# Retention's last values in one narrow run, folded squares for the last keys and queries, masks in other buffers

## The chip, the cores and the metric

The kernel runs on one core of a Trainium2 chip. The metric is the device time of one execution in microseconds (us). Before the change it is 1216.12 us, the median of three runs (1215.96 to 1216.55).

## The reference

An encoder of two layers on 512 tokens of width 1024, all in float32. In each layer one projection of the normed input feeds two groups of heads: eight heads of retention in both directions, and four heads of differential attention. Both are projected back and added, and a SwiGLU network follows. What this change touches:

```python
# retention, per head, in its closed form
# out[t] = sum_{s<=t} gf^(t-s) (q_t.k_s) v_s + sum_{s>t} gb^(s-t) (q_t.k_s) v_s
ret = rms_norm(ret, ret_norm_g[l]) * jax.nn.silu(rg)      # per head of 64

# differential attention: keys and queries are normed per head of 64
dqn = rms_norm(dq, dq_norm_g[l]) * DIFF_HEAD_DIM ** -0.5
dkn = rms_norm(dk, dk_norm_g[l])
...
x = x + concat([ret, da]) @ w_out[l]
```

## The kernel before

Activations lie transposed: 128 features on the partitions, 512 tokens along the free dimension. Most products are made of three passes in a rounded float32 format: an operand is split into a rounded part `hi` and a rest `lo`, and `mm3` (L220) issues hi*hi, hi*lo and lo*hi. The splits cost a cast on ScalarE (ACT) and a subtraction on VectorE (DVE).

Retention works on pairs of heads, 0 to 3, in two chunks of 256 tokens. For a pair, `prepare` weighs queries and keys by the decay and stacks their parts (with moves issued by SP); `scores` multiplies queries and keys of each chunk into the `sc` banks (L581) and multiplies them by the decays into mask tiles `sm` (L587); `state` makes the 64x64 state between chunks (L502); `cross` applies it to the queries (L514); `values` multiplies masks and values (L525); `norm` norms the result, multiplies it by the gate and splits it into a part of the mix, which the output projection's second half reads. `state`, `cross` and `values` are plain float32 matmuls, and `state` and `values` are narrow: they use 64 columns of the array, two at a time side by side.

The order in this stage is written out as the string `STEPS` (L38): `a`, `b` and `n` with a number are `prepare`, `scores` and `norm` of a pair, `k` is `state`, `v` and `V` are `cross` and `values`, `+` joins several into one run, `h` is the end of the last attention head, and `-` takes the next piece of other work (projections, then the output projection's first half from the attention heads). `together` chains the matmuls of a run one behind the other with order edges, all crosses first. With `V` the weighing of that pair's queries is put behind the other things that the run needs. `scores` puts its matmuls behind the run before it, and pair 3's decays behind the first matmul of the run before. The string and these edges give rank and order; a planner in the framework then places each instruction on its engine, by rank, as its inputs and buffers come free, and may move later work forward.

The four attention heads run before that stage. `heads` gives sixteen turns (four a head), and `weave` puts one piece of a list between two turns: keys and queries of heads 2 and 3 (`project_k`, `project_q`), the four gates, and the first retention projections. A `yield` in a piece hands over to the next turn. `qk_tile` norms keys or queries: `square_sums` squares the tile, splits it, and adds over each head's 64 rows with two matmuls (L140 and L141) against a matrix of ones. `fold` and `folded_sums` do the same for an attention head's output with one matmul (L162): an accumulating DMA on POOL adds the upper 64 rows of squares to the lower 64, and hi and lo of the sums are stacked in one tile.

Buffers are pools by tag: `ah` has 4, `h` has 8 (the normed input of the layer, and later that of the second norm), `w` has 12, `mix` 20.

Of the kernel before, what the change touches and what calls it, by code (L numbers as in the profile page):

```python
# [8 lines left out]
F32 = mybir.dt.float32  # L9
F32R = mybir.dt.float32r  # L10
AF = mybir.ActivationFunctionType
ALU = mybir.AluOpType

P = 128
D = 1024
T = 512
DEPTH = 2
KT = D // P
HD = 64
# [15 lines left out]
PLAIN = FFN[0][1]  # L35
BEGUN, LASTS = (2, 9, 10, 20, 21), (18,)

STEPS = "a0 h - b0 - a1 - - - - k0+k1 b1 - - a2 - - a3 V0+v1+k2+k3 b2 b3 n0 n1 - - - V2 n2 - - v3 - n3"  # L38


NW, NQK, NMIX, NAH, NHL = 12, 11, 20, 4, 3
# [4 lines left out]
PRM_AG, PRM_FG, PRM_RG, PRM_QG, PRM_KG, PRM_DG = 0, 16, 32, 34, 36, 38  # L46
# [9 lines left out]
def encoder_kernel(ctx: ExitStack, tc: tile.TileContext, xT, xg, wfirst, wsingle, wvv, wout, wgu, wdn, wds, prm, lam, cst, outT):  # L56
    nc = tc.nc
# [4 lines left out]
    tpool = ctx.enter_context(tc.tile_pool(name="tpool", bufs=1))  # L62
# [5 lines left out]
    def nm(s):  # L68
        uid[0] += 1
        return f"{s}{uid[0]}"  # L70

    def big(s, dt=F32, tag="w", bufs=NW):
        return tpool.tile([P, T], dt, tag=tag, name=nm(s), bufs=bufs)
# [17 lines left out]
    consts, first_part = {}, []  # L91

    def f32(ap):
        return ap.bitcast(F32)
# [18 lines left out]
    prm_sb = cpool.tile([P, PRM_N], F32, name="prm_sb")  # L113
# [23 lines left out]
    def column_sums(ps, w, src):  # L137

        hi, lo = split(src, "w", NW)
        sums[1] = nc.tensor.matmul(ps, w, hi, start=True, stop=False).ins.name  # L140
        sums[0] = nc.tensor.matmul(ps, w, lo, start=False, stop=True).ins.name  # L141
# [3 lines left out]
    def square_sums(ps, w, src):  # L145
        sq = big("sq")
        nc.scalar.activation(sq, src, AF.Square)
        column_sums(ps, w, sq)
        return sq
# [8 lines left out]
    def folded_sums(ps, w, sq):  # L158
        parts = big("hl", F32R)
        nc.scalar.copy(parts[:HD], sq[:HD])  # L160
        nc.vector.tensor_tensor(parts[HD:], sq[:HD], f32(parts[:HD]), op=ALU.subtract)
        nc.tensor.matmul(ps, w, parts, start=True, stop=True)  # L162

    def round_ones():
        o = big("ones")
# [71 lines left out]
    def split(src, tag, bufs):  # L237
        hi, lo = pair() if tag == "h" else [big(n, F32R, tag, bufs) for n in ("hi", "lo")]
        casts[0] = nc.scalar.copy(hi, src).ins.name
        splits[0] = nc.vector.tensor_tensor(lo, src, f32(hi), op=ALU.subtract).ins.name  # L240
        return hi, lo
# [3 lines left out]
    def rsqrt(out, src, scale):  # L245

        func(out, src, AF.Ln, bias=eps_sb, scale=scale)
        func(out, out, AF.Exp, scale=-0.5)
# [84 lines left out]
    def layer(l, n1, h, x_src, first_raw):  # L333
# [27 lines left out]
        lg, nlgb, lamn, gq, gd, wk, rs = (consts[k] for k in ("lg", "nlgb", "lamn", "gq", "gd", "wk", "rs"))  # L361
# [43 lines left out]
                k.append((hi, lo))  # L405
            return k

        def qk_tile(u, col, early, stack):
            ss = aux_bank()
            sq = square_sums(ss, consts["bones_r"], u)  # L410
            rsqrt(sq, ss, 1.0 / HD)

            nc.vector.scalar_tensor_tensor(u, u, col, sq, op0=ALU.mult, op1=ALU.mult)
            nc.scalar.activation(sq, sq, AF.Square, scale=HD ** -0.5)
            nc.vector.scalar_tensor_tensor(sq, ss, HD * EPS, sq, op0=ALU.add, op1=ALU.mult)
            nc.vector.scalar_tensor_tensor(u, sq, 3.0, u, op0=ALU.subtract, op1=ALU.mult)
            return stack(u, *(("qk", NQK) if early else ("mix", NMIX)))
# [54 lines left out]

        ret, run = [dict() for _ in range(4)], [None, None]

        def together(steps):
            names = [n for t in steps for n in (ret[int(t[1])]["state" if t[0] == "k" else "values"])]
            ins = [i for t in steps if t[0] != "k" for i in cross(int(t[1]))]
            ins += [i for t in steps for i in (state if t[0] == "k" else values)(int(t[1]))]
            for i, before in zip(ins, [names] + [[i.name] for i in ins]):
                for name in before:  # L480
                    tc.add_manual_dep(i, name, order, reason="one run of plain matmuls")
            if steps[0][0] == "k":
                tc.add_manual_dep(ins[0], scored[0], order, reason="one run of plain matmuls")
            run[:] = ins[-1].name, ins[0].name
            first = [ret[int(t[1])]["weigh"] for t in steps if t[0] == "V"][:1]
            for i in first:
                for name in names:
                    if name != i.name:
                        tc.add_manual_dep(i, name, order, reason="one run of plain matmuls")
# [69 lines left out]
        def scores(pr):  # L559
            lgc = lambda d, hh: lg[:, l * 16 + d * 8 + 2 * pr + hh : l * 16 + d * 8 + 2 * pr + hh + 1]  # L560
            lgm = lambda hh: nlgb[:, l * 8 + 2 * pr + hh : l * 8 + 2 * pr + hh + 1]
            qs, ks = ret[pr]["stacks"]
            both = []

            for hh in range(2):
                arg = big("arg")
                i = nc.scalar.activation(arg[:, :384], signed, AF.Copy, scale=lgm(hh))
                if run[1] and pr == 3:
                    tc.add_manual_dep(i.ins, run[1], order, reason="decays behind the run")
                nc.vector.scalar_tensor_tensor(arg[:, :384], signed, lgc(0, hh), arg[:, :384], op0=ALU.mult, op1=ALU.min)  # L570
                func(arg[:, :384], arg[:, :384], AF.Exp)
                both.append(bass.AP(arg.tensor, arg.offset, [arg.ap[0], [P, 2], [1, C]]))
            s = ret[pr]["s"] = []
            for c in range(2):
                ps = [sc_bank() for _ in range(2)]
                for j in range(2):
                    for hh in range(2):
                        out = ps[hh][:, (1 - j) * C : (2 - j) * C]
                        sb, tb = slice((2 * c + j) * P, (2 * c + j + 1) * P), slice(c * C, (c + 1) * C)
                        for part in range(2):  # L580
                            i = nc.tensor.matmul(out, ks[hh][part][:, sb], qs[hh][:, tb], start=part == 0, stop=part == 1)  # L581
                            if run[0]:
                                tc.add_manual_dep(i.ins, run[0], order, reason="one run of plain matmuls")
                scored[0] = i.ins.name
                sm = tpool.tile([P, 2, T], F32, tag="ah", name=nm("sm"), bufs=NAH)
                for hh in range(2):
                    i = nc.vector.tensor_tensor(  # L587
                        sm[:, hh].rearrange("p (j t) -> p j t", j=2), ps[hh].rearrange("p (j t) -> p j t", j=2), both[hh], op=ALU.mult
                    )
                    ret[pr]["values"].append(i.ins.name)  # L590
                s.append(sm)

        def norm(pr):
            o, ss = ret[pr]["o"], aux_bank()
            sq = square_sums(ss, consts["bones_r"], o)
            rsqrt(sq, ss, 1.0 / HD)
            nc.vector.scalar_tensor_tensor(sq, o, prm_sb[:, PRM_RG + l : PRM_RG + l + 1], sq, op0=ALU.mult, op1=ALU.mult)
            nc.vector.tensor_tensor(sq, sq, gates[pr], op=ALU.mult)
            mix[pr] = split(sq, "mix", NMIX)

        kgc = consts["gk"][:, l : l + 1]
        dv = [[], []]
        rv = [[], []]
        rks, rqs, gates = [], [], []
# [60 lines left out]
        def project_k(m):  # L665
            ps = project("dk", m)
            if m != 2:
                yield
            u = big("u")
            nc.vector.tensor_tensor(u, ps, rstd, op=ALU.mult)  # L670
            if m == 2:
                yield
            k[m] = qk_tile(u, kgc, False, stack_two)

        def project_q(m):
            ps = project("dq", m)
            yield
            u = big("u")
            nc.vector.tensor_tensor(u, ps, rstd, op=ALU.mult)
            q[m] = qk_tile(u, gq[:, l, m : m + 1], False, stack_one)  # L680

        def project_gate(m):
            t = big("rgt", tag="rn", bufs=4)
# [5 lines left out]
        q, k = [None] * 4, [None] * 4  # L689
# [49 lines left out]
        n2, h2, x = Norm(), [], []  # L739
# [38 lines left out]
        )  # L778
        for step in STEPS.split():
            if step == "-":  # L780
                next(fill)
            elif step == "h":
                next(lasthead[0])
            elif step[0] in "kvV":
                together(step.split("+"))
            else:
                {"a": prepare, "b": scores, "n": norm}[step[0]](int(step[1]))
        for _ in fill:
# [10 lines left out]
        n3, h3 = Norm(), []  # L799
# [195 lines left out]
        a1 = PLAIN  # L995
# [45 lines left out]
        a0, a1 = FFN[-1]  # L1041
# [30 lines left out]
    n, h, raws = Norm(), [], []  # L1072
# [7 lines left out]
    for l in range(DEPTH):  # L1080
        if l:
            raws = [load_chunk(wfirst[l, c]) for c in range(4)]
        n, h = layer(l, n, h, xT if l == 0 else xscr, raws)
# [89 lines left out]
```

## Time and profile before

| | before |
|---|---|
| median of three runs | 1216.12 us |
| profiled execution, its time | 1216.29 us |
| profiled execution, its span | 1214.5 us |
| TensorE matmuls (PE), busy | 1210.0 us, 7631 instructions |
| VectorE (DVE), busy | 961.1 us |
| ScalarE (ACT), busy | 744.8 us |
| GpSimd (POOL), busy | 99.2 us |

The span is the time from the first to the last instruction in the trace; the execution's time has 1.8 us more around it. In the order of time a row gives start, duration, engine, line, operation, what it writes and reads, shape and count; consecutive instructions of one kind share a row. A matmul's shown duration is longer than its distance to the next one, since matmuls overlap. 128*64 in a matmul's row means 128 rows and 64 columns of the array. A row of a group ends with busy time, the mean time of one in ns, and the idle time of the engine ahead of it. The stage of retention lies at about 190 to 260 us in layer 0 and at about 795 to 860 us in layer 1.

### The profile page before, as it was taken

To read this page: it belongs to the slowest core of one execution; us is meant where nothing else is said; L and a number is where in the kernel's file an instruction comes from. 1 tells how busy PE (TensorE), PEld (TensorE's weight loads), DVE (VectorE), ACT (ScalarE), POOL (GpSimd) and SP (SyncE) were. 2 spreads that over 40 slices of the span, in tenths; PEclk is the share of its full clock that TensorE was granted. 3 is DMA by queue.
4 is the path that set the end of the run, shared out by engine and by line. 5 is a ranking of instruction groups with operands and counts; after the bars stand their busy time and mean duration, and the time that the engine had idled before them with its cause. 6 is when DMAs were issued, how large, how long until landed. Compare 5 with 4: busy or idle time off the path is not lost.

```text
span 1214.5 us, 19995 instructions
## 1 busy us (share of the span) xinstructions
PE 1210.0 (100%) x7631; PEld 1083.2 (89%) x7631; DVE 961.1 (79%) x1585; ACT 744.8 (61%) x1300; POOL 99.2 (8%) x116
## 2 busy tenths in 40 slices
PE   9999999999999999999999999999999999999998
PEld 7888888888899999999888888887888999999997
DVE  6899777778978888876648996777789788898763
ACT  6877667655456556655548776676554565666541
POOL 1000001210011111110000000011100011111100
PEclk9999999999999999999999999999999999999999
DMA  7222224773176786782532222357532757867822
GB/s 268 87 70 76 89 75 126 155 188 104 64 170 166 173 214 155 181 218 84 169 113 79 78 74 74 92 144 163 144 122 73 181 144 190 207 161 182 202 79 96
DMA packets 71520, 164.87 MB, mean 136 GB/s; under 512 B 6912, under 2 KB 17408, under 8 KB 71424
## 3 DMA queue, kind: packets, MB, share of 16 engines
q1 hardware_dynamic: 54064, 133.00, 35.5%
q0 software_dynamic: 16928, 30.15, 15.0%
q8 instruction: 60, 0.98, 0.3%
q10 hardware_dynamic: 432, 0.44, 0.1%
q14 instruction: 36, 0.29, 0.1%
HBM read 153.34 MB, written 4.19 MB: 130 GB/s over the span
## 4 chain that ended last, share of the span: by engine, by line
PE 99%; DMA 0%; ACT 0%; DVE 0%; issue 0%
PE acc L913 23%; PE sc L913 17%; PE acc L221 11%; PE acc L222 11%; PE acc L223 11%; PE o L223 3%; PE o L222 3%; PE o L221 3%; PE sc L221 3%; PE sc L222 3%; PE sc L223 3%; PE sc L432 2%; PE sc L581 1%; PE o L525 1%; PE aux L448 1%; PE aux L140 1%
## 5 line engine op out<-in xcount | busy, mean ns | idle before, releaser
L208 ACT CAST hi<-raw 128x1024 fp32r<-128x1024 f32 (+2 forms) x117 | 115.8, 993 | 121.9 <-PE sc L222 39.3
L214 DVE TENSOR_TENSOR lo<-raw,hi 128x1024 fp32r<-128x1024 f32 (+2 forms) x118 | 135.4, 1150 | 36.6 <-ACT hi L208 35.9
L221 PE MATMUL acc<-h,hi 128*128 128x512 f32 (+1 forms) x344 | 134.3, 393 | 0.5 <-ACT h L232 0.4
L223 PE MATMUL acc<-h,lo 128*128 128x512 f32 (+1 forms) x344 | 134.1, 390 | 0.0
L222 PE MATMUL acc<-h,hi 128*128 128x512 f32 (+1 forms) x344 | 133.8, 389 | 0.0
L913 PE MATMUL acc<-hi,hi 128*128 128x256 f32 x432 | 122.5, 284 | 0.0
L913 PE MATMUL acc<-hi,lo 128*128 128x256 f32 x432 | 122.2, 283 | 0.0
L913 PE MATMUL acc<-lo,hi 128*128 128x256 f32 x432 | 122.2, 283 | 0.0
L870 DVE TENSOR_TENSOR lo<-s,hi 128x1024 fp32r<-128x1024 f32 (+1 forms) x78 | 89.0, 1141 | 32.7 <-ACT hi L869 32.4
L870 DVE TENSOR_TENSOR lo<-raw,hi 128x1024 fp32r<-128x1024 f32 (+1 forms) x78 | 89.0, 1141 | 30.9 <-ACT hi L869 26.9
L869 ACT CAST hi<-s 128x1024 fp32r<-128x1024 f32 (+1 forms) x78 | 76.7, 983 | 51.5 <-PE acc L913 37.1
L869 ACT CAST hi<-raw 128x1024 fp32r<-128x1024 f32 (+1 forms) x78 | 76.5, 981 | 39.0 <-PE acc L913 18.8
L913 PEld LDWEIGHTS acc<-lo,hi 128*128 128x128 f32 x432 | 82.9, 192 | 0.1
L913 PEld LDWEIGHTS acc<-hi,hi 128*128 128x128 f32 x432 | 82.9, 192 | 0.1
L913 PEld LDWEIGHTS acc<-hi,lo 128*128 128x128 f32 x432 | 82.9, 192 | 0.0
L221 PEld LDWEIGHTS acc<-h,hi 128*128 128x128 f32 x344 | 64.6, 188 | 14.4 <-PE o L223 0.7
L223 PEld LDWEIGHTS acc<-h,lo 128*128 128x128 f32 x344 | 64.6, 188 | 13.2
L891 POOL DMA_DIRECT2D s<-in_wgu x36 | 43.3, 1203 | 404.7 <-DMA s<-in_wgu 186.3
L222 PEld LDWEIGHTS acc<-h,hi 128*128 128x128 f32 x344 | 64.7, 188 | 12.8 <-DVE h L234 0.2
L913 PE MATMUL sc<-b,s 128*128 128x256 f32 x480 | 69.3, 283 | 0.0
L913 PEld LDWEIGHTS sc<-b,s 128*128 128x128 f32 x480 | 62.8, 192 | 0.0
L107 ACT ACTIVATE sc<-sc,mx 128x512 f32<-128x512 f32 x64 | 46.1, 721 | 22.8 <-DVE mx L436 22.5
(276 smaller groups left out, 3533.8 us busy)
## 6 DMA issues: line engine op xcount, KB each, us to landing
s<-in_wgu SPq DMA_DIRECT2D x54, 512.0 KB, 5.5
s<-in_wgu POOLq DMA_DIRECT2D x36, 512.0 KB, 7.5
raw<-in_wgu SPq DMA_DIRECT2D x34, 512.0 KB, 5.3
raw<-in_wsingle SPq DMA_DIRECT2D x32, 512.0 KB, 3.5
raw<-in_wvv SPq DMA_DIRECT2D x18, 512.0 KB, 3.5
raw<-in_wgu SPq DMA_DIRECT2D x36, 256.0 KB, 3.6
s<-in_wds SPq DMA_DIRECT2D x24, 384.0 KB, 3.4
raw<-in_wout SPq DMA_DIRECT2D x16, 512.0 KB, 3.7
```

Source lines behind the costliest of these rows:

```text
L107: i = nc.scalar.activation(out, src, f, **kw).ins
L140: sums[1] = nc.tensor.matmul(ps, w, hi, start=True, stop=False).ins.name
L208: c = nc.scalar.copy(hi[:, s], raw[:, s])
L214: nc.vector.tensor_tensor(lo[:, s], raw[:, s], f32(hi[:, s]), op=ALU.subtract)
L221: first = nc.tensor.matmul(out, L[0], R[0], start=start, stop=False)
L222: nc.tensor.matmul(out, L[0], R[1], start=False, stop=False)
L223: nc.tensor.matmul(out, L[1], R[0], start=False, stop=stop)
L432: nc.tensor.matmul(ps, q[m][:, t], k[m][part], start=part == 0, stop=part == 1)
L869: last_cast[0] = nc.scalar.copy(hi, raw).ins.name
L870: last_split[0] = nc.vector.tensor_tensor(lo, raw, f32(hi), op=ALU.subtract).ins.name
L891: nc.gpsimd.dma_start(sums, blocks[:, 0::3], accum_op=ALU.add)
L913: mm = nc.tensor.matmul(ps[:, t], L[x1], R[x2], start=start and k + i == 0, stop=k == n // P - 1 and i == 2, skip_group_check=True)
```

## The change

It has four parts.

- `STEPS`: pair 2's scores (`b2`) move ahead of the first run `V0+v1+k2+k3`, and the values of pairs 2 and 3 (`V2` and `v3`, two runs with other work between them) become one run `V2+v3` behind pair 3's scores, the norms of pairs 0 and 1, and three pieces of the output projection. The mark `!` says that a run is held behind the last score matmul emitted so far; before, that held for the run `k0+k1` alone.
- The squares of keys and queries of head 3 (`m == 3`): `fold_each` squares, and two accumulating DMAs on POOL add rows 32 to 63 to rows 0 to 31 of each head's 64; `each_parts` casts, subtracts, and two moves on SP put the rest `lo` into the freed half. One matmul makes the sums. Each of these tiles gets two more `yield`s.
- Pairs 2 and 3 take their mask tiles `sm` from tag `h` instead of `ah`.
- In `norm`, the gate is multiplied by the result and its weight ahead of the root; one product remains behind it.

```diff
-STEPS = "a0 h - b0 - a1 - - - - k0+k1 b1 - - a2 - - a3 V0+v1+k2+k3 b2 b3 n0 n1 - - - V2 n2 - - v3 - n3"
+STEPS = "a0 h - b0 - a1 - - - - !k0+k1 b1 - - a2 - - a3 b2 !V0+v1+k2+k3 b3 n0 n1 - - - !V2+v3 n2 - - - n3"
...
+    def fold_each(src):
+
+        sq = big("sq")
+        nc.scalar.activation(sq, src, AF.Square)
+        for b in (0, HD):
+            nc.gpsimd.dma_start(sq[b : b + 32], sq[b + 32 : b + HD], accum_op=ALU.add)
+        return sq
+
+    def each_parts(sq):
+        parts, lo = big("hl", F32R), big("lo", F32R)
+        nc.scalar.copy(parts, sq)
+        nc.vector.tensor_tensor(lo, sq, f32(parts), op=ALU.subtract)
+        for b in (0, HD):
+            nc.sync.dma_start(f32(parts[b + 32 : b + HD]), f32(lo[b : b + 32]))
+        return parts
...
-        def qk_tile(u, col, early, stack):
+        def qk_tile(u, col, early, stack, folded=None):
             ss = aux_bank()
-            sq = square_sums(ss, consts["bones_r"], u)
+            if folded:
+                sq, parts = folded
+                nc.tensor.matmul(ss, consts["bones_r"], parts, start=True, stop=True)
+            else:
+                sq = square_sums(ss, consts["bones_r"], u)
...
-        def together(steps):
+        def together(steps, behind=False):
...
-            if steps[0][0] == "k":
+            if behind:
                 tc.add_manual_dep(ins[0], scored[0], order, reason="one run of plain matmuls")
...
-                sm = tpool.tile([P, 2, T], F32, tag="ah", name=nm("sm"), bufs=NAH)
+                sm = tpool.tile([P, 2, T], F32, name=nm("sm"), **(dict(tag="ah", bufs=NAH) if pr < 2 else dict(tag="h", bufs=8)))
...
         def norm(pr):
             o, ss = ret[pr]["o"], aux_bank()
             sq = square_sums(ss, consts["bones_r"], o)
+            nc.vector.scalar_tensor_tensor(gates[pr], o, prm_sb[:, PRM_RG + l : PRM_RG + l + 1], gates[pr], op0=ALU.mult, op1=ALU.mult)
             rsqrt(sq, ss, 1.0 / HD)
-            nc.vector.scalar_tensor_tensor(sq, o, prm_sb[:, PRM_RG + l : PRM_RG + l + 1], sq, op0=ALU.mult, op1=ALU.mult)
             nc.vector.tensor_tensor(sq, sq, gates[pr], op=ALU.mult)
...
-            if m == 2:
+            folded = None
+            if m == 3:
+                sq = fold_each(u)
                 yield
-            k[m] = qk_tile(u, kgc, False, stack_two)
+                folded = sq, each_parts(sq)
+                yield
+            elif m == 2:
+                yield
+            k[m] = qk_tile(u, kgc, False, stack_two, folded)
...
-            q[m] = qk_tile(u, gq[:, l, m : m + 1], False, stack_one)
+            folded = None
+            if m == 3:
+                sq = fold_each(u)
+                yield
+                folded = sq, each_parts(sq)
+                yield
+            q[m] = qk_tile(u, gq[:, l, m : m + 1], False, stack_one, folded)
...
-            elif step[0] in "kvV":
-                together(step.split("+"))
+            elif step[0] in "!kvV":
+                together(step.strip("!").split("+"), step[0] == "!")
```

## The prediction

> **What bounds the kernel now.** I read the page first (busy time, clock, chain), then the waits of TensorE, then the order of time around the stage that the change touches.
>
> ```profile
> span 1214.5 us, 19995 instructions
> PE 1210.0 (100%) x7631; PEld 1083.2 (89%) x7631; DVE 961.1 (79%) x1585; ACT 744.8 (61%) x1300; POOL 99.2 (8%) x116
> PEclk9999999999999999999999999999999999999999
> PE 99%; DMA 0%; ACT 0%; DVE 0%; issue 0%
> ```
>
> ```profile
> PE aux L118 <- PEq L1165: 0.8, 1, 0.8
> PE acc L221 <- ACT h L232: 0.4, 1, 0.4
> ```
>
> The chain that ended last is TensorE for 99%, the clock is granted in full in every slice, and in the whole program TensorE waits twice, both times at the start. So only two things can change the time: work that TensorE no longer has, and a wait that it gets. The busy column does not give the price of a matmul, because matmuls overlap; I take it from start to start in the order of time. I show layer 0; the same stage of layer 1 lies some 603 us later.
>
> This is the run of plain matmuls of pairs 0 and 1 with the states of pairs 2 and 3:
>
> ```profile
> 200.32 0.39 PE L223 MATMUL acc<-h,lo 128*128 128x512 f32 x1
> ...
> 221.77 0.39 PE L223 MATMUL acc<-hi,lo 128*128 128x512 f32 x1
> 222.00 1.89 PE L514 MATMUL o<-wq,rs 128*128 128x256 f32 x8
> 223.82 3.67 PE L525 MATMUL o<-sm,rv 128*64 128x256 f32 x32
> 227.32 1.10 PE L502 MATMUL aux<-rv,kw 128*64 128x64 f32 x32
> 228.35 0.39 PE L581 MATMUL sc<-q,khi 128*128 128x256 f32 x1
> ```
>
> These are one pair of squares' sums, then the values of pair 2 between two halves of pair 3's scores, then those of pair 3:
>
> ```profile
> 231.70 0.40 PE L140 MATMUL aux<-hi,bones_r 128*128 128x512 f32 x1
> 231.94 0.39 PE L141 MATMUL aux<-lo,bones_r 128*128 128x512 f32 x1
> 232.17 0.39 PE L222 MATMUL acc<-lo,hi 128*128 128x512 f32 x1
> ...
> 237.76 1.03 PE L514 MATMUL o<-wq,rs 128*128 128x256 f32 x4
> 238.72 1.95 PE L525 MATMUL o<-sm,rv 128*64 128x256 f32 x16
> 240.59 0.39 PE L581 MATMUL sc<-q,khi 128*128 128x256 f32 x1
> 240.82 0.28 PE L581 MATMUL sc<-q,klo 128*128 128x256 f32 x1
> 240.94 0.28 PE L581 MATMUL sc<-q,khi 128*128 128x256 f32 x1
> ...
> 241.72 1.03 PE L514 MATMUL o<-wq,rs 128*128 128x256 f32 x4
> 242.40 0.58 PE L140 MATMUL aux<-hi,bones_r 128*128 128x512 f32 x1
> 242.82 0.39 PE L221 MATMUL sc<-hi,hi 128*128 128x512 f32 x1
> ...
> 243.52 0.39 PE L221 MATMUL sc<-hi,hi 128*128 128x512 f32 x1
> 243.83 1.95 PE L525 MATMUL o<-sm,rv 128*64 128x256 f32 x16
> 245.71 0.50 PE L221 MATMUL sc<-hi,hi 128*128 128x512 f32 x1
> 246.04 0.40 PE L222 MATMUL sc<-lo,hi 128*128 128x512 f32 x1
> 246.28 0.40 PE L223 MATMUL sc<-hi,lo 128*128 128x512 f32 x1
> ```
>
> A wide matmul of 512 columns has a pitch of 0.23 us (231.94 to 232.17), one of 256 columns 0.12 us (240.82 to 240.94). Around a narrow run (128*64) the pitch is worse: 0.31 us from the last wide matmul into the run (243.52 to 243.83), and 0.33 us for the first wide one behind it (245.71 to 246.04), against 0.23 each.
>
> **The change part by part.**
>
> *One run for pairs 2 and 3.* Today's price: pair 2 takes from 237.76 to 240.94 less two score matmuls at 0.12, so 3.18 - 0.24 = 2.94 us. Pair 3: four crosses with a sum behind them, 242.82 - 241.72 - 0.23 = 0.87; entering 0.31 - 0.23 = 0.08; values 245.71 - 243.83 = 1.88; first wide matmul behind them 0.33 - 0.23 = 0.10; together 2.93. Sum 5.87 us. The merged run has the eight crosses and 32 values of the first run, 1.82 (222.00 to 223.82) and 3.50 us (223.82 to 227.32), and then an exit: 0.11 on the first wide matmul (0.23 - 0.12 at 240.59), and whatever the last values cost at the end of a narrow run, between 0 and 0.12 (1.87 us for 16 against half of 3.50 for 32). That is 5.43 to 5.55, a gain of 0.32 to 0.44 us; I take 0.35, nearer the lower end, as the 16 values of either run show the same excess. Two layers: 0.70 us.
>
> *Folded squares of the last keys and queries.* Two tiles in each of two layers lose one of two sums of 512 columns: 4 x 0.23 = 0.92 us. ACT and DVE keep their counts (square, cast, subtraction). New are two accumulating DMAs on POOL and two moves on SP for each tile. The nearest rows are the head's fold on POOL and the shifts of half a tile on SP:
>
> ```profile
> L155 POOL DMA_DIRECT2D sq<-sq x6: 807/814/984, 102.0 to 769.5; - x6
> DMA to landing us min/median/max: 2.8/2.9/5.1
> q<-qlo SPq DMA_DIRECT2D x16, 128.0 KB, 4.1
> ```
>
> The new chain from square to sum is two issues of 0.81, a landing of 2.9, a cast and a subtraction of about 0.65 each, and a landing of 4.1: 9.9 us, at most 12.1 with the longest landing. Behind the waiting POOL issues stand only the zero fills of the keys' stacks and the next head's fold; behind SP's moves stand the next weight loads. What hides it is the distance from the last queries' sum to the last head, which uses them:
>
> ```profile
> 112.78 0.40 PE L140 MATMUL aux<-hi,bones_r 128*128 128x512 f32 x1
> ...
> 150.55 0.39 PE L432 MATMUL sc<-khi,q 128*128 128x512 f32 x1
> ```
>
> There are 37.8 us, and two chains one after the other take 20 to 24. The four new turns also push the gate projections back by four of the sixteen turns of the heads; the projections behind them fill TensorE as before. I take 0. If the cover is gone, a sum that comes late by the spread of the landings costs 2.2 us, four of them 8.8.
>
> *The later masks in the input's buffers.* The last matmul that reads the normed input stands at 200.32, so the four mask tiles find free buffers 20 us before any of them is written. No cost. The next input in these buffers is written only once pair 3 is mixed, which is behind the values that read the masks.
>
> *Pair 2's scores ahead of the first run.* This is the part that can cost. The run is now held behind the second half of pair 2's scores. That half needs the score banks back from the masks of the first half, and these need pair 2's decays:
>
> ```profile
> 218.76 1.29 DVE L587 TENSOR_TENSOR sm<-sc,arg 128x512 f32<-128x512 f32 x2 [0.89 <-PE sc L581]
> ...
> 222.51 1.12 ACT L567 ACTIVATE arg<-cst_sb,prm_sb 128x384 f32<-128x384 f32 x2
> 223.54 1.03 ACT L208 CAST hi<-raw 128x1024 fp32r<-128x1024 f32 x1
> ...
> 224.96 1.76 ACT L107 ACTIVATE arg<-arg 128x384 f32<-128x384 f32 x4
> ```
>
> The banks are free at 218.76 + 1.29 = 220.05, so the first half (8 x 0.12 = 0.95 us) fits before 222.00 + 0.95 = 222.95. The first two decays are done at 224.96 + 0.88 = 225.84, or 224.7 once pair 3's first two decay steps (1.12 us at 222.51), which stay behind the run, no longer stand ahead of them. Two masks (1.29) end at 226.0 and the second half at 227.0. So between 222.95 and 226.0 TensorE lives on the last two of the eight tiles of the output projection's first half, 6 and 7, whose weights are cast at 223.54 + 1.03 = 224.57, and 1.12 us earlier, 223.45, without the same two steps. Each tile is twelve matmuls of 0.23, 2.7 us, so they cover the rest. The hole is 223.45 - 222.95 = 0.5 us. The bounds for a layer: 0, if the planner keeps an earlier tile back for it; 226.0 - 222.95 = 3.1 us, if tiles 6 and 7 do not come first. I take 0.5, the value by the rows as they stand: 1.0 us for two layers.
>
> *The norm.* The gate is multiplied in ahead of the root, so one DVE step moves off the chain from pair 3's values to the mix. The order of its end today:
>
> ```profile
> 251.79 0.74 DVE L597 SCALAR_TENSOR_TENSOR sq<-o,prm_sb,sq 128x512 f32<-128x512 f32 x1
> ...
> 254.00 0.69 DVE L240 TENSOR_TENSOR lo<-sq,hi 128x512 fp32r<-128x512 f32 x1 [0.74 <-ACT hi L239]
> ```
>
> ```profile
> 255.88 0.61 PE L221 MATMUL sc<-hi,hi 128*128 128x512 f32 x2
> ```
>
> The mix is ready at 254.69 and first used at 255.88: 1.2 us of room, which grows by 0.74. It hides nothing on TensorE today, so it gains 0; it is cover for the later values.
>
> **The sum.** -0.92 - 0.70 + 1.0 = -0.6 us. The profiled execution took 1216.29 us, 1.8 of them outside its span; by it the changed kernel takes 1215.7. It stands 0.17 above the median of 1216.12, so the forecast is 1215.5 us, or 0.05% less.
>
> **The rivals.**
>
> *No hole at all.* TensorE has no wait anywhere in this stage today, which speaks for it. Then the time is 1216.12 - 1.62 = 1214.5.
>
> *The first run waits in full (slower).* If tiles 6 and 7 stand behind the run, TensorE idles 3.1 us a layer: 1214.5 + 6.2 = 1220.7. It is slower by over 0.2% (2.4 us) once the wait passes 2.0 us a layer. For it: the run has higher rank in the written order than the projection. Against: the projection was already moved up past scores today (the one before these two ends at 222.00).
>
> *The mix comes late.* Pair 2's 2.94 us now stand directly ahead of pair 3's values. If pair 3's masks are no earlier than today, the mix is 2.94 - 0.74 - 1.2 = 1.0 us late a layer: 1214.5 + 2.0 = 1216.5. Against: of the four halves of scores that stand behind the run today only two remain, so these masks should be earlier.
>
> *The folds come late.* All four late by 2.2 us: 1223.3. The head's fold lands before its matmul each time today. [...]
>
> **How the numbers follow.** Chances: the forecast's 0.5 us hole 0.35, no hole 0.25, late mix 0.15, full wait of the first run 0.15, late folds 0.05, something that gains beyond 1.6 us 0.05. A difference under 0.2% cannot be told from none with this kernel. The first three are within it (0.75); the waits and folds are slower (0.20); more gain is 0.05, since TensorE has no wait to give back. The range runs from 1213.9, the upper gain of the merged run (0.44 twice, -1.8) and some 0.4 of scatter, to 1218.6, a wait of 2.0 us a layer. The likeliest case alone lies within 1214.5 to 1216.5.
>
> **What would show it.** Three narrow runs a layer instead of four; eight crosses and 32 values in one piece, with a single slow wide matmul behind them; two fewer hi/lo sums of 512 columns a layer. Right for the hole: a pitch of about 0.7 us ahead of a tile of the output projection near 222 us. Wrong: a wait of TensorE for a mask of pair 2, a landing or a mix, or the first run starting at once.

## The result, and the profile after

The changed kernel takes 1214.65 us (median of 22 runs, 1214.19 to 1215.52), the kernel before on the same chip 1216.32 us (22 runs, 1215.96 to 1217.02). The ratio is 0.9986, 95% interval 0.9980 to 0.9992: a gain of 1.67 us, outside the scatter but below the 0.2% that the forecast counted as a difference. The forecast was 1215.5; the time is nearer to that of its rival without a hole (1214.5).

The page of the changed kernel (busy time and share by engine) and the waits of TensorE (us in total, times, longest):

```profile
span 1212.6 us, 20029 instructions
PE 1208.5 (100%) x7627; PEld 1083.0 (89%) x7627; DVE 958.8 (79%) x1585; ACT 747.6 (62%) x1300; POOL 106.2 (9%) x124
```

```profile
PE aux L118 <- PEq L1197: 0.8, 1, 0.8
```

TensorE has four matmuls fewer, and no wait but the one at the start. The stage in layer 0, in TensorE's order of time (start, duration; L534 are crosses, L545 values, L522 states, L601 scores):

```profile
220.77 0.28 PE L601 MATMUL sc<-q,klo 128*128 128x256 f32 x1
220.89 1.89 PE L534 MATMUL o<-wq,rs 128*128 128x256 f32 x8
222.71 3.67 PE L545 MATMUL o<-sm,rv 128*64 128x256 f32 x32
226.21 1.10 PE L522 MATMUL aux<-rv,kw 128*64 128x64 f32 x32
227.25 0.39 PE L601 MATMUL sc<-q,khi 128*128 128x256 f32 x1
...
238.42 0.62 PE L237 MATMUL sc<-hi,hi 128*128 128x512 f32 x2
238.88 1.89 PE L534 MATMUL o<-wq,rs 128*128 128x256 f32 x8
240.69 3.67 PE L545 MATMUL o<-sm,rv 128*64 128x256 f32 x32
244.30 0.50 PE L238 MATMUL sc<-lo,hi 128*128 128x512 f32 x1
244.63 0.39 PE L239 MATMUL sc<-hi,lo 128*128 128x512 f32 x1
```

The last of pair 2's score matmuls starts at 220.77 and the first run follows one pitch later, at 220.89, 1.1 us earlier than before, where those scores still lay behind it. The merged run is one piece: crosses 1.81 us (238.88 to 240.69), values 3.61 (to 244.30), and one slow wide matmul behind them, 0.33 against 0.23.

The groups of the sums of squares (count, then busy us and mean ns), and the landings of the folds' DMAs (count, size, median us from issue to landing):

```profile
L140 PE MATMUL aux<-hi,bones_r 128*128 128x512 f32 x20 | 7.9, 397 | 0.0
L141 PE MATMUL aux<-lo,bones_r 128*128 128x512 f32 x20 | 7.9, 395 | 0.0
L428 PE MATMUL aux<-hl,bones_r 128*128 128x512 f32 x4 | 1.7, 435 | 0.0
```

```profile
sq<-sq POOLq DMA_DIRECT2D x8, 64.0 KB, 3.3
hl<-lo SPq DMA_DIRECT2D x8, 64.0 KB, 2.6
```

L140 and L141 had 24 each before; four folded sums (L428) take the place of four pairs. The issues of the new folds on POOL (shortest, median and longest in ns):

```profile
L169 POOL DMA_DIRECT2D sq<-sq x8: 763/1016/1142, 82.2 to 704.9; - x8
```

What moved besides is the beginning of the stage. The last fold of an attention head in layer 0, on POOL, first before, then after:

```profile
167.28 0.81 POOL L155 DMA_DIRECT2D sq<-sq  x1 [24.96 <-ACT ah L451]
```

```profile
158.37 0.81 POOL L155 DMA_DIRECT2D sq<-sq  x1 [29.91 <-ACT ah L471]
```

And pair 2's first two decay steps on ScalarE, first before, then after, where the rows of L802 tell of the tiles of the output projection's first half (a copy there ends a tile):

```profile
220.25 1.12 ACT L567 ACTIVATE arg<-cst_sb,prm_sb 128x384 f32<-128x384 f32 x2
```

```profile
213.03 1.12 ACT L587 ACTIVATE arg<-cst_sb,prm_sb 128x384 f32<-128x384 f32 x2
...
220.13 0.59 ACT L802 COPY x<-acc 128x512 f32<-128x512 f32 x1 [0.42 <-PE acc L239]
...
232.77 0.59 ACT L802 COPY x<-acc 128x512 f32<-128x512 f32 x1
235.89 0.59 ACT L802 COPY x<-acc 128x512 f32<-128x512 f32 x1 [0.24 <-PE acc L239]
239.35 0.57 ACT L802 COPY x<-acc 128x512 f32<-128x512 f32 x1
```

The heads reach their last fold 8.9 us earlier, the decays are 7.2 us earlier, and three of the eight tiles are still to come behind the first run. The rest of this document is about why.

### The profile page after: what moved, and what is told of

It is laid out like the page before. It is cut to its first block, busy times and chain, and to the rows that moved or that the text cites. A ratio compares the mean times of both kernels' runs of the same rounds, so it can differ in the third digit from the quotient of the medians.

```text
span 1212.6 us, 20029 instructions
## 1 busy us (share of the span) xinstructions
PE 1208.5 (100%) x7627; PEld 1083.0 (89%) x7627; DVE 958.8 (79%) x1585; ACT 747.6 (62%) x1300; POOL 106.2 (9%) x124
## 4 chain that ended last, share of the span: by engine, by line
PE 100%; DVE 0%; issue 0%
PE acc L945 23%; PE sc L945 17%; PE acc L237 11%; PE acc L239 11%; PE acc L238 11%; PE o L239 3%; PE o L238 3%; PE o L237 3%; PE sc L238 3%; PE sc L237 3%; PE sc L239 3%; PE sc L452 2%; PE sc L601 1%; PE o L545 1%; PE aux L468 1%; PE o L534 1%
## 5 line engine op out<-in xcount | busy, mean ns | idle before, releaser
L945 PE MATMUL acc<-h,hi 128*128 128x256 f32 x288 | 53.7, 283 | 0.0
```

The source lines that it names most:

```text
L945: mm = nc.tensor.matmul(ps[:, t], L[x1], R[x2], start=start and k + i == 0, stop=k == n // P - 1 and i == 2, skip_group_check=True)
```

## The experiments

Every time below stands beside the kernel before on the same chip, with the ratio and its 95% interval. Where the interval contains 1, the times alone do not tell the difference from none; what is said of it then rests on the traces too.

**The steps alone.** The changed kernel without the folds and without their turns:

```diff
-            if m == 3:
+            if m == 9:
```

(in `project_k` and in `project_q`).

> The change without the folds: keys and queries of head 3 are squared, split and summed with two matmuls as before, and get no extra turns; order, merged run, masks and norm are those of the change. Theory (the time is TensorE's own work, and it waits nowhere): only the merged run is gained, 0.70 us, so 0.7 below the kernel before and 0.9 above the changed kernel, about 1215.6 us where before is 1216.3. On why the forecast hole ahead of the first run did not open: if the new place of pair 2's scores in the written order moved pair 1's and pair 2's chains forward by itself, pair 2's decays begin near 213 us in layer 0 here too, and no hole shows. If instead the folds' extra turns moved the stage forward, pair 2's decays begin near 220 us here, and a hole of about 0.5 us a layer opens: 1216.6 us.

Measured: 1221.36 against 1216.11 us, 1.0048 (1.0035 to 1.006), five runs. TensorE's waits, and its order of time:

```profile
PE sc L237 <- ACT hi L255: 2.9, 2, 1.4
...
PE sc L601 <- DVE sm L607: 0.4, 2, 0.2
...
PE aux L141 <- DVE lo L256: 0.3, 2, 0.2
```

```profile
229.37 1.89 PE L534 MATMUL o<-wq,rs 128*128 128x256 f32 x8
...
238.03 0.49 PE L141 MATMUL aux<-lo,bones_r 128*128 128x512 f32 x1 [0.16 <-DVE lo L256]
238.75 0.39 PE L601 MATMUL sc<-q,khi 128*128 128x256 f32 x1 [0.23 <-DVE sm L607]
...
241.52 0.73 PE L237 MATMUL sc<-hi,hi 128*128 128x512 f32 x2 [1.43 <-ACT hi L255]
242.09 1.97 PE L534 MATMUL o<-wq,rs 128*128 128x256 f32 x8
```

```profile
229.64 0.58 ACT L802 COPY x<-acc 128x512 f32<-128x512 f32 x1
```

The decays of pair 2 begin at 220.3 us, but there is no hole ahead of the first run, and neither expected time came. All eight tiles of the output projection are used up there (the last copy is at 229.64, just after the run began at 229.37), so behind the run nothing is left to lie between the scores, the norms and the mix. The waits there, 3.6 us in both layers together, are for the mix (2.9), for masks and for the squares of a norm. So the steps by themselves make the kernel slower by 5.25 us, although the merged run is in them too.

**The folds alone**, with their turns, in the old order (the diff is `STEPS`, the mask tag and `norm` put back):

> The folds alone, with their extra turns; the order string, masks and norm are those of before. Theory: four sums of 0.23 us go, 0.92 us less than before, about 1215.4 us. Rival (folds come late): a sum that waits for its landings by up to 2.2 us each, so up to 1215.4 + 8.8. On the stage's order: if the extra turns move the stage forward, the first narrow run (states of pairs 0 and 1) begins near 196 us as in the changed kernel; if not, near 203 us as before (less 0.5).

Measured: 1215.31 against 1216.11 us, 0.9994 (0.9985 to 1.0003), eleven runs. That is 0.80 less; four sums of 0.23 are 0.92. No wait is new, and the first narrow run starts at 196.1 us in layer 0, so the stage moves forward here as in the changed kernel. The two halves of the change, measured apart, would add up to +4.45 us; together they are -1.67. The parts are not independent, and the question is what the folds bring to the steps.

**The turns alone with the steps.** The changed kernel, where the `m == 3` branches hold nothing but the two `yield`s:

```diff
             if m == 3:
-                sq = fold_each(u)
                 yield
-                folded = sq, each_parts(sq)
                 yield
```

> The changed kernel without the folds but with their turns: keys and queries of head 3 get two empty turns each, and are squared, split and summed with two matmuls. Theory (the extra turns lower the rank of the projections behind them, the heads end some 9 us earlier, retention's chain starts earlier, and its projections are left as filler; the folds themselves only take four sums away): no waits, the changed kernel's order, and 4 x 0.23 = 0.92 us above it: 1215.6 us. Rival (the folds' own chain, not the turns, moves the stage): the waits of the steps alone come back, about 1221.4 us.

Measured: 1215.32 against 1216.10 us, 0.9994 (0.9985 to 1.0003), eleven runs. This is the only wait of TensorE:

```profile
PE aux L118 <- PEq L1193: 0.8, 1, 0.8
```

Against the steps alone only four empty turns a layer are new, and they take 6.0 us away. Three tiles stand behind the first run here too.

**The folds without their turns**, with the steps:

```diff
                 sq = fold_each(u)
-                yield
                 folded = sq, each_parts(sq)
-                yield
```

> The changed kernel with the folds but without their four extra turns (fold, split and norm are emitted at once). Theory of the turns: the third head's fold is issued near 167 us in layer 0 as before, the output projection's first half is used up ahead of the first run, TensorE waits behind it as with the steps alone: 1221.4 - 0.9 = 1220.5 us. Rival (the folds move it): 1214.65 us; and if a sum waits for its landings because nothing stands between, up to 2.2 us more for each of four.

Measured: 1217.1 against 1216.10 us, 1.0007 (0.9998 to 1.0016), eleven runs: between the two theories. Two tiles are left behind its first run, and TensorE's waits other than the start's come to 0.8 us:

```profile
PE acc L237 <- DVE rgt L713: 0.8, 2, 0.4
```

```profile
91.01 0.50 PE L237 MATMUL acc<-h,hi 128*128 128x512 f32 x1 [0.34 <-DVE rgt L713]
```

Both of these lie among the attention heads (91.0 and 693.9 us) and are for a gate, so two tiles were enough to leave no wait behind the first run. What the stage of retention still loses is in longer distances between matmuls: summed over 185 to 262 and over 785 to 870 us, they exceed the usual pitch of each kind by some 0.9 us a layer more than in the changed kernel (an estimate from the starts in the two traces). So the folds close a part of the loss without the turns.

**The turns alone in the kernel before** (four `yield`s and nothing else):

> The kernel before with nothing but the four empty turns (two behind the projection of head 3's keys, two behind that of its queries). Theory (the time is TensorE's work, and the turns only change what is left as filler): the stage moves forward as in the changed kernel (pair 1's scores near 202 us in layer 0 instead of 209), and the time stays at 1216.1 us. Rival (the turns gain by themselves, or starve the heads of filler): a difference of over 0.5 us.

Measured: 1216.62 against 1216.42 us, 1.0003 (0.9994 to 1.0011), eleven runs. The turns gain nothing where there is no wait to close. They move the stage all the same: the run `k0+k1` starts at 196.8 us in it, at 203.6 before, at 196.3 in the changed kernel, and at 203.6 with the steps alone. So the turns by themselves move the stage, with the folds or without.

**The shorter sum alone.** The steps without folds and turns, and the matmul of the squares' rests (L141) left out for the last keys and queries; the sums of these squares are then of rounded squares only:

```diff
+            elif short:
+                sq = big("sq")
+                nc.scalar.activation(sq, u, AF.Square)
+                hi, lo = split(sq, "w", NW)
+                nc.tensor.matmul(ss, consts["bones_r"], hi, start=True, stop=True)
             else:
                 sq = square_sums(ss, consts["bones_r"], u)
```

> The steps alone, no folds and no extra turns, and the second matmul of the sums of the last keys' and queries' squares (the one of the rests) left out: the squares' sums have only their rounded parts, 4 matmuls of 0.23 us less in all, with the old chain (cast and subtraction, no DMA, no move). It asks why the folds without their turns took 3.3 us of the hole's cost away beyond their own 0.92. Theory A: TensorE's shorter work ahead of the heads is enough, the planner then places the projections otherwise: about 1217.1 as with the folds without turns. Theory B: the folds' longer chain does it, since sums that come later let other work pass: then the hole stays as with the steps alone, and the time is 1221.4 - 0.9 = 1220.4.

Measured: 1225.37 against 1216.12 us, 1.0071 (1.0057 to 1.0085), five runs. Both theories fell: with 0.92 us less work the kernel is 4.0 us slower than the steps alone. Most of the 4.0 us is clock: the profiled execution, which is the median one, has a stretch at half rate in each layer, 1.7 us lost in each (the windows below for layer 0; in layer 1 the granted clock is 0.58 from 850 to 854 us, and 0.42 x 4 is 1.7). The median execution of the steps alone has a granted clock of 1.000. The waits, the order of time, the rows of the output projection's last tile (here L807), and the windows (busy PE, PEld, DVE, ACT, POOL with counts; granted clock, DMA share, GB/s):

```profile
PE o L539 <- DVE wq L568: 5.3, 2, 2.6
PE sc L606 <- ACT khi L399: 1.0, 1, 1.0
```

```profile
241.68 2.50 PE L539 MATMUL o<-wq,rs 128*128 128x256 f32 x8 [2.64 <-DVE wq L568]
244.11 4.81 PE L550 MATMUL o<-sm,rv 128*64 128x256 f32 x32
```

```profile
226.23 0.57 ACT L807 COPY x<-acc 128x512 f32<-128x512 f32 x1
...
238.72 0.59 ACT L807 COPY x<-acc 128x512 f32<-128x512 f32 x1
```

```profile
242.00:244.00 2.00, 2.00 (x8) 1.28 (x6) 1.92 (x4) 1.24 (x2) 0.00 (x0) 0.76 1.14 218
244.00:246.00 2.00, 2.00 (x11) 1.13 (x12) 0.27 (x1) 0.00 (x0) 0.91 (x2) 0.50 1.02 297
246.00:248.00 2.00, 2.00 (x20) 1.28 (x18) 0.13 (x1) 0.73 (x2) 1.23 (x2) 0.89 0.85 151
```

One tile is left behind the first run here, which starts at 226.84. It bridges the norms and the scores, and then pair 2's weighed queries (`wq`), which VectorE makes behind pair 3's masks, are waited for in one piece of 2.64 us, directly ahead of the merged run. After that wait the clock is halved for a while: the crosses take 2.43 us instead of 1.81, the values 1.1 more. The other waits, 1.2 us, lie ahead of the first run, at 208.7 and 816.3 us. So shorter work by itself does not explain the folds without turns, and which tiles stay behind does not follow smoothly from the amount of work.

**The old order by the string.** Two changes of `STEPS` alone. First the values of pairs 2 and 3 in two runs again, which lets other work come between them:

```diff
-... n0 n1 - - - !V2+v3 n2 ...
+... n0 n1 - - - !V2 v3 n2 ...
```

> The changed kernel with the values of pairs 2 and 3 as two runs one right behind the other (cross and values of pair 2, then cross and values of pair 3), all else as changed. It has one change more from wide to narrow and back in each layer, and nothing moves far. Theory (each narrow run pays for its entry and exit): 0.32 to 0.44 us a layer, so 0.7 us above the changed kernel, about 1215.35 us. Rival (the gain of the merged run was its place in the order, not the switch): no difference, 1214.65 us.

Measured: 1215.31 against 1216.11 us, 0.9993 (0.9984 to 1.0002), eleven runs: a loss of 0.66 us on the medians of the two kernels, or of 0.87 with each beside its own kernel before, where 0.70 was expected. The intervals of the two kernels overlap, so this agrees with the expected size without settling it. Then pair 2's scores behind the first run again, with the mark kept:

```diff
-... a3 b2 !V0+v1+k2+k3 b3 ...
+... a3 !V0+v1+k2+k3 b2 b3 ...
```

> The changed kernel with pair 2's scores written behind the first run again, as before; the merged run of pairs 2 and 3, folds, masks and norm stay. Theory one (the room of the mix, 1.2 us before plus 0.74 from the norm, is enough or nearly so): 1214.65 us, at most 0.5 above. Rival (the merged run needs the earlier scores): pair 3's last masks end near 242.9 us as before, the merged run ends some 2.9 us later than pair 3's values did, and the mix is 1.0 us late a layer: 1214.65 + 2.0 = 1216.65 us, with TensorE waiting ahead of the output projection's second half.

Measured: 1219.24 against 1216.11 us, 1.0026 (1.0015 to 1.0037), seven runs, some 4.6 us above the changed kernel, and so above both expectations. TensorE waits mostly behind the merged run, for the squares of its norm, and not for the mix, as the rival had it:

```profile
PE aux L140 <- ACT hi L255: 2.6, 2, 1.3
...
PE sc L237 <- DVE sm L607: 0.6, 2, 0.3
```

With the first run at 216.0 instead of 220.9, the tiles kept back are used up behind it, and none is left for the last norms. Filler can be missing at either end of the stage.

**The norm put back** to the old order of its two products:

> The changed kernel with the norm's old order (the gate and the weight behind the root). Theory (the mix has room to spare, as pair 3's values end at about the same time and nothing waits on it): no difference, 1214.65 us. Rival (the shorter chain is needed): up to 0.74 us a layer, 1216.1 us.

Measured: 1214.65 against 1216.10 us, 0.9987 (0.9979 to 0.9996), eleven runs: no difference from the changed kernel.

**More folds.** Three tries to fold the keys and queries of head 2 as well. First `m >= 2` in both functions, which by the code adds three pieces a layer (one for the keys, which had a turn already, and two for the queries), more than the sixteen turns hold:

> The changed kernel with keys and queries of head 2 folded as well, with two extra turns each. Theory (the time is TensorE's work): four more sums of 0.23 us go, 1214.65 - 0.92 = 1213.7 us. Rival (nineteen turns of fillers do not fit into sixteen, or head 2 waits for its keys and queries, whose sums stood only some 2 to 27 us ahead of it): a wait at the start of the third head, or the projections left over behind the heads, above 1214.65 us.

Measured: 1241.23 against 1216.10 us, 1.0197 (1.0179 to 1.0215), four runs. Then a generator that advances several of the four pieces in one turn, meant to leave each projection in its place, for keys and queries of heads 2 and 3 and, without the fold of head 2's keys, for three of these four (the second cut is against the first):

```diff
-                [project_k(2), project_q(2), project_k(3), project_q(3)]
+                [tiles("k2|k2 q2|k2 q2 k3|k2 q2 k3|q2 k3|k3 q3|q3|q3|q3")]
```

```diff
-                [tiles("k2|k2 q2|k2 q2 k3|k2 q2 k3|q2 k3|k3 q3|q3|q3|q3")]
+                [tiles("k2|k2 q2|q2 k3|q2 k3|q2 k3|k3 q3|q3|q3|q3")]
```

> The changed kernel with keys and queries of head 2 folded too, but with their waiting turns woven between the projections that follow, so that each projection stays in the turn that it has in the changed kernel. Theory (four more sums of 0.23 us go; with the projections in place TensorE keeps its filler in the first turns): 1214.65 - 0.92 = 1213.7 us. Rival (two or three folded tiles at once hold too many of the twelve work buffers, or head 2 waits): waits of TensorE between 70 and 120 us, and a time above 1214.65 us.

> The same weave, but of head 2 only the queries are folded, not the keys. Theory: two more sums go, 1214.65 - 0.46 = 1214.2 us. Rival (work buffers): above 1214.65 us, with fewer waits than with both.

Measured: 1221.26 against 1216.42 us, 1.0043 (1.003 to 1.0055), five runs, and 1227.73 against 1216.42, 1.0092 (1.0078 to 1.0106), five runs. In all three the expected gain missed, and the times are above 1214.65 us as their rivals said. That the work buffers are the reason is not shown, and three woven folds have more waits than four, not fewer. The longest waits, first of the three more pieces, then of four woven folds, then of three:

```profile
PE o L237 <- ACT ah L471: 3.9, 4, 1.3
```

```profile
PE sc L452 <- DVE mx L456: 5.6, 6, 1.4
```

```profile
PE o L534 <- DVE wq L563: 5.3, 2, 2.6
PE sc L452 <- DVE mx L456: 2.7, 2, 1.4
```

The waits for the softmax lie mostly in the first turns of the heads, from 66 to 94 us in layer 0. In 60 to 100 us the changed kernel keeps TensorE busy for 39.97 of 40 us with VectorE at 39.57; in the kernel with three more pieces it is 36.10, at a granted clock of 0.87:

```profile
60.00:100.00 40.00, 39.97 (x198) 32.92 (x197) 39.57 (x83) 30.93 (x61) 3.11 (x5) 1.00 0.25 74
```

```profile
60.00:100.00 40.00, 36.10 (x155) 28.58 (x154) 34.99 (x78) 26.69 (x56) 4.62 (x6) 0.87 0.27 69
```

A likely reading is that pieces which wait for a fold in these turns issue no projection, so that the softmax (`mx`, `ah`, `al`) is waited for; it was not tested apart. With three folds the stage of retention is hit too, by the same wait for `wq` as above, and again one tile stands behind the first run. The kernel with three more pieces shows the same within one run: in layer 0 one tile stands behind the first run and `wq` is waited for 2.6 us, in layer 1 three tiles and no such wait. A fold gains 0.23 us (the pitch of the sum that goes; the folds alone gained 0.80 for four); these kernels lose 4.8 to 25 us against the kernel before.

## Why the prediction was right or wrong

*What bounds it.* Right: TensorE had no wait to give back but two at the start, and every kernel slower than before by more than 0.2% shows new waits of TensorE.

*The merged run.* Right. 1.81 + 3.61 + 0.10 is 5.52 us against 5.87: 0.35 a layer, the value taken. The entry into the crosses cost nothing (238.42 to 238.88 is two pitches), and the step from them into the narrow values is within the 1.81.

*The folds.* Right in count (four sums of 0.23), and hidden as forecast: landings of 3.3 and 2.6 us in the median where 2.9 and 4.1 were taken, and no wait of TensorE for them. The issues took 0.76 to 1.14 us (row of L169) where 0.81 was taken. The cover shrank: the queries' sum starts at 126.60 and the last head's first score at 143.18 us, 16.6 us where the prediction counted on 37.8. It was enough, and the rival of late folds did not occur.

*The masks and the norm.* Right at zero; the norm put back changes nothing. The masks were not tried by themselves, so for them only the sum speaks.

*The hole ahead of the first run.* This step failed: 0.5 us a layer was taken, and the changed kernel has none. The lower bound that the step itself gave, an earlier tile kept back, is what happened, but with a cause that the prediction had priced at nothing. It said of the four new turns that "the projections behind them fill TensorE as before". It then kept pair 1's scores and pair 2's decays at the times of before (217.8 and 220.25). In fact the turns put the pieces behind them later among the heads' work. The heads reach their last fold 8.9 us earlier, retention's chain begins earlier (196.3 against 203.6), the decays run at 213.0, and three tiles of the output projection remain behind the first run as filler. The steps with empty turns and without (1215.32 and 1221.36 us) differ in the turns alone, so it is shown that the turns take the loss away. That they do it through the tiles left over is read from the traces; no run changed the tiles alone.

With the old times, as the steps alone have them, the placing of the loss was wrong as well. The prediction saw the danger ahead of the run if tiles 6 and 7 stand behind it. It was the reverse: they stood ahead of it, nothing was left behind it, and the loss lay behind the run. From the pitches of the order of time it is 3.1 us in layer 0. That this comes near the rival's 3.1 us is chance; the rival's mechanism, a first run that waits, was seen in none of these kernels.

*The sum.* Without the term of the hole it is -1.62; measured are -1.67 on the medians and -1.80 on the two profiled executions (1216.29 and 1214.49 us). That the forecast of 1215.5 came within 0.9 us is in part luck: a loss of the steps (5.25 us alone) and its removal by the turns (6.0 us) were both left out of it, and they cancelled.

What stays open: the folds without turns lose 2.45 us against the changed kernel, where the theory had the whole loss of the steps. Their heads reach the last fold at 165.5, 1.8 us earlier than with the steps alone, and two tiles stay behind. Of the 2.45, the two waits for a gate among the heads are 0.75, and the longer distances in the stage some 0.9 a layer. Less work on TensorE is not the reason by itself, since the shorter sum brought no gain: even without the time lost to the clock (two stretches of 1.7 us, last section) it stands some 0.6 us above the steps alone. Whether it is the folds' longer chain or where the planner puts the other pieces was not separated.

## What to carry to other kernels

On an engine that is full, as here, moving a step cost nothing by its own length (the norm put back moves one of 0.74 us: 1214.65 us with and without); it cost when it changed which work is left over to lie beside the next chain. So look at the filler: at each point where a chain begins, how many independent tiles are still to come. With `b2` ahead of the first run, the waits of TensorE behind that run were, per layer: none with three tiles, none with two (one kernel), 2.64 us with one (the same wait for `wq` in three kernels), 1.8 us with none (one kernel). The count alone is no rule: one tile was worse than none, and with pair 2's scores behind the run again four tiles were used up too early, with 1.6 us of waits a layer. And do not read the due times of a step from the profile of before when the same change also moves the rank of the work ahead of it; measure such parts together and apart, since a loss of 5.25 and a gain of 0.80 made a gain of 1.67 here.

## What the hardware showed

The granted clock fell to half (0.50 in a window of 2 us) after short waits, and not each time. In the kernel with the shorter sum, one wait of 2.64 us was followed by 0.76, 0.50 and 0.89 of the clock in the three windows above: (0.24 + 0.50 + 0.11) x 2 us / 0.5 = 3.4 us at half rate (the middle window shows the half). With three woven folds the same wait of 2.64 us was not followed by any loss (a granted clock of 1.00 from 236 to 252 us):

```profile
244.19 1.99 PE L534 MATMUL o<-wq,rs 128*128 128x256 f32 x8 [2.64 <-DVE wq L563]
246.12 3.67 PE L545 MATMUL o<-sm,rv 128*64 128x256 f32 x32
```

With the steps alone, layer 0 kept its clock (1.00 from 236 to 250 us) after the waits shown, the longest of them 1.43 us, and layer 1 lost it after the same waits:

```profile
844.00:848.00 4.00, 2.57 (x12) 1.97 (x12) 3.77 (x7) 2.26 (x5) 1.82 (x2) 0.84 1.02 328
848.00:852.00 4.00, 4.00 (x22) 2.79 (x22) 0.89 (x2) 0.25 (x1) 1.79 (x2) 0.74 1.02 182
```

That is (0.16 + 0.26) x 4 us / 0.5 = 3.4 us again, an estimate that takes the 0.50 of the kernel with the shorter sum as the rate, since these windows of 4 us do not show it. Of the five executions of the steps alone, the two with a granted clock of 0.999 took 1222.65 and 1222.68 us, the three with 1.000 took 1220.97 to 1221.36. So waits of 2.64 us, or of 1.43 us among smaller ones, stood ahead of such a stretch in some executions or layers and not in others; what decides it is not shown. In these two kernels a stretch cost 1.3 to 1.7 us on top of the wait (the lowest and highest difference between those executions; 0.85 x 2 us and 0.42 x 4 us from the windows). More can be lost: in the kernel with three more pieces, the clock averaged 0.87 over the 40 us from 60 to 100 us, 0.13 x 40 = 5.2 us lost, in one stretch or in several.
